# Turning activation blocks for the next product: transposes issued three steps later, the last feed-forward chunk by the tensor engine, one mLSTM block by DRAM

## The chip, the cores and the metric

The kernel runs on one core of one Trainium2 chip. A core has a tensor engine (PE) for matrix products, a vector engine (DVE), a scalar engine (ACT), GpSimd (POOL) and a sync engine (SP) that here only issues transfers. The metric is the time of one execution in microseconds (us), as the median of repeated runs. The kernel before takes 1747.4 us, and its three runs lie between 1746.92 and 1747.4 us.

## The reference

One decoder layer on 256 tokens of width 2048, in fp32. Every product below is against weights that are read once from memory.

```python
def hybrid_mixer(h, ...):
    mq, mk, mv, mo, mi, mf, dq, dk, dv, gm, gd = split_in(h @ w_in)
    ...                                              # conv and silu on mq, mk
    hm = jax.nn.sigmoid(mo) * head_rmsnorm(mlstm_chunkwise(q, k, v, ig, lf), m_norm_w)
    hd = head_rmsnorm(diff_attention(dq, dk, dv, lam), d_norm_w) * (1.0 - lam_init)
    y = jax.nn.sigmoid(gm) * (hm @ w_bm) + jax.nn.sigmoid(gd) * (hd @ w_bd)
    return y @ w_out
def swiglu(h, w_gate, w_up, w_down):
    return (jax.nn.silu(h @ w_gate) * (h @ w_up)) @ w_down
def reference(x, ...):
    x = x + hybrid_mixer(rmsnorm(x, attn_norm_w), ...)
    x = x + swiglu(rmsnorm(x, ffn_norm_w), w_ffn_gate, w_ffn_up, w_ffn_down)
    return rmsnorm(x, final_norm_w)
```

## The kernel before

**Products.** A number is kept as two parts, hi and lo, and a product is three matmuls: hi by hi, hi by lo, lo by hi (`three`, L175; its lines L177 to L179 are the matmuls of the profile). Weights arrive by DMA in pieces of 1 MB (`wr`, four buffers). ACT casts half a piece to its hi part (`wh`, L331, or L478 in the plain products) and DVE subtracts to get the lo part (`wl`, L335 or L479); both rings have five buffers, and a split is written into the program four units ahead of the product that reads it (`AHEAD`). Some products come in pairs that share seven instead of eight block products (`Pair`, L341; the banks P1 to P8): `bd` (hd by w_bd), `wo` (y by w_out), `fgu` (gate and up) and `fd` (down). DVE adds up raw weights for those (L323), and `quarters` (L407) puts the outputs together with DVE (L410).

**Turned activations.** A product reads its activations with features on the partitions. They are computed with tokens on the partitions, so each block of 512 features (a chunk) is turned before the product that reads it. The chunk is kept in a `Split` (`hmT`, `yT`, `x1T`, and `gT0`, `gT1`, `gT2` for the three parts of the feed-forward, which have 4, 4 and 3 chunks). `across_task` (L202) chooses the way by the chunk's kind:

- a kind in `TURN` (L46) goes by `turn_task` (L249): two DVE stream transposes of 32x32 blocks (L255), one POOL DMA to DRAM (L260), four POOL DMAs back (L265), then the hi part by ACT (L278, or L282 and L283 where a scale is applied) and the lo part by DVE (L279 or L284);
- any other kind goes by `transpose_task` (L210): a wait of two steps, four PE transposes of 128x128 into a bank (L187), hi by ACT (L190, or L196 with a scale), lo by DVE (L191 or L199), a wait of two steps, and the same for the second half.

Before, the PE way is taken by `hm0` (the first mLSTM block, which `bm` reads much later), by `ylast` (chunks 2 and 3 of y, read by wo0), by `x1last` (chunks 2 and 3 of x1, read by fgu0), and by `glast` (chunk 2, the last, of gT2, read by fd20). The last chunk (3) of gT0 and of gT1, read by fd00 and fd10, has the kind `g` and goes by DRAM (L1140).

**What sets the order.** The whole program is written out by hand, engine by engine, and each engine runs its list in order. Side work is held in generators of class `Side` (L89). `side.tick()` moves each of them on by one step; `Pair.run` (L383) ticks after every six matmuls of a pair, so a step is six matmuls of the main product. Generators of one lane run one after another; `ylast`, `x1last` and `glast` chunks share the lane `tr`. Before a product reads a chunk, `side.until` ticks as often as it takes for the chunk's last instruction to be in the program. The number after `yield` in `transpose_task` is thus what places the PE transposes between the matmuls.

Of the kernel before, what the change touches and what calls it, by code (L numbers as in the profile page):

```python
# [42 lines left out]
)  # L43
N_WARM = (6, 2)
SHORT = set()
TURN = {"q0", "k0", "hm1", "hm2", "hm3", "dq", "dk", "hd0", "hd1", "hd2", "hd3", "y", "x1", "g"}  # L46


@with_exitstack
def hybrid_block(ctx, tc, x, attn_norm_w, w_in, conv_w, conv_b, b_igate, b_fgate, mlstm_norm_w,  # L50
# [17 lines left out]
    def c4(shape, name, dt=F32):  # L68
        return c4p.tile(shape, dt, tag="c4", name=name)
# [8 lines left out]
    def t2(shape, name, dt=F32):  # L78
        return smp.tile(shape, dt, tag="t2", name=name, bufs=N_T2)
# [9 lines left out]
    class Side:  # L89
# [10 lines left out]
        def across(self, lane, kind, *rest):  # L100

            gen = across_task(kind, *rest)
            if kind in TURN and kind not in SHORT:
                self.spawn(gen)
# [28 lines left out]
    side = Side()  # L133
# [47 lines left out]
    def transpose_half(src, dst, g, pr, scale_col=None):  # L181

        hi, lo = dst.hi[g], dst.lo[g]
        ps = bank("ps_tr", (P, 2, S))
        for j in range(2):
            for tt in range(TT):
                nc.tensor.transpose(ps[:, j, tt * P:(tt + 1) * P], src(tt, 2 * pr + j), ident)  # L187
        if scale_col is None:
            h = hi[:, 2 * pr:2 * pr + 2]
            nc.scalar.copy(out=h, in_=ps)  # L190
            nc.vector.tensor_tensor(out=lo[:, 2 * pr:2 * pr + 2], in0=ps, in1=h.bitcast(F32),  # L191
                                    op=ALU.subtract)
        else:
            for j in range(2):
                k = 2 * pr + j
                nc.scalar.activation(out=hi[:, k], in_=ps[:, j], func=AF.Identity, scale=scale_col(4 * g + k))  # L196
            for j in range(2):
                k = 2 * pr + j
                nc.vector.scalar_tensor_tensor(out=lo[:, k], in0=ps[:, j], scalar=scale_col(4 * g + k),  # L199
                                               in1=hi[:, k].bitcast(F32), op0=ALU.mult, op1=ALU.subtract)  # L200

    def across_task(kind, tile, dst, g, scale_col=None, rate=2):  # L202
        if kind in SHORT:
            yield from turn_short_task(tile, dst, g, scale_col, rate)
        elif kind in TURN:
            yield from turn_task(tile, dst, g, scale_col, rate)
        else:
            yield from transpose_task(lambda tt, j: tile[:, tt, j * P:(j + 1) * P], dst, g, scale_col)

    def transpose_task(src, dst, g, scale_col=None):  # L210
        yield 2
        dst.alloc(g)
        transpose_half(src, dst, g, 0, scale_col)
        yield 2
        transpose_half(src, dst, g, 1, scale_col)
        dst.ready[g] = True
# [11 lines left out]
    def turn_short_task(src, dst, g, scale_col=None, rate=2):  # L228
        yield 1
        t = c4([P, 4, S], "turned")  # L230
        yield from turn(src, t, rate)
        hi, lo = dst.alloc(g)
        for k in range(0, 4, 2):
            if scale_col is None:
                nc.scalar.copy(out=hi[:, k:k + 2], in_=t[:, k:k + 2])
                nc.vector.tensor_tensor(out=lo[:, k:k + 2], in0=t[:, k:k + 2], in1=hi[:, k:k + 2].bitcast(F32),
                                        op=ALU.subtract)
            else:
                for j in (k, k + 1):
                    sc = scale_col(4 * g + j)  # L240
                    nc.scalar.activation(out=hi[:, j], in_=t[:, j], func=AF.Identity, scale=sc)
                    nc.vector.scalar_tensor_tensor(out=lo[:, j], in0=t[:, j], scalar=sc, in1=hi[:, j].bitcast(F32),
                                                   op0=ALU.mult, op1=ALU.subtract)
            if k == 0:
                yield
        yield
        dst.ready[g] = True
# [159 lines left out]
    def quarters(pair):  # L407

        def op(o, i0, i1, op_):
            nc.vector.tensor_tensor(out=o, in0=i0, in1=i1, op=op_)  # L410
        ps = pair.banks
        yield from pair.after("P3", 2)
        s3, u, v, x = (t2([P, 512], f"q{i}") for i in range(4))
        nc.scalar.copy(out=s3, in_=ps["P3"])
        yield from pair.after("P6", 2)
        op(u, s3, ps["P6"], ALU.subtract)
        op(v, u, ps["P4"], ALU.add)
        yield
        op(x, v, ps["P5"], ALU.subtract)
        op(u, ps["P5"], u, ALU.subtract)  # L420
        for t, c, b, o, op_ in ((0, 0, "P1", s3, ALU.add), (1, 0, "P7", v, ALU.subtract),
                                (0, 1, "P2", u, ALU.add), (1, 1, "P8", x, ALU.add)):
            yield from pair.after(b, 2)
            op(o, ps[b], o, op_)
            yield t, c, o
# [357 lines left out]
    def conv_task(tok, ft0, dst):  # L783
# [3 lines left out]
        dst.alloc(0)  # L787
        if dst.name in TURN:
            t = c4([P, 4, S], "turned")
            yield from turn(tok, t)  # L790
        for pr in range(2):
            y = t2([P, 2, S], "cv")
            if dst.name in TURN:
                ps = t[:, 2 * pr:2 * pr + 2]
# [278 lines left out]
    x1 = []  # L1073
# [52 lines left out]
    def gate_up_post(gT, i):  # L1126
        def task(pair):
            g = c4([P, TT, 512], "g")
            for got in quarters(pair):
                if got is None:  # L1130
                    yield
                    continue
                t, c, q = got
                yield
                if c == 0:
                    nc.scalar.activation(out=g[:, t], in_=q, func=AF.Silu, scale=r2(t))
                else:
                    nc.vector.scalar_tensor_tensor(out=g[:, t], in0=q, scalar=r2(t), in1=g[:, t],
                                                   op0=ALU.mult, op1=ALU.mult)
            side.across("tr", "g" if i < 2 or len(gT.hi) > 3 else "glast", g, gT, i, None, 4)  # L1140
        return task

    ss2 = small([P, TT, 4], "ss2", bufs=1)
# [106 lines left out]
    for pi, (f0, f1) in enumerate(parts):  # L1250
        gT = Split(f1 - f0, f"gT{pi}", {0})
# [81 lines left out]
```

## Time and profile before

| what | value |
|---|---|
| median of three runs | 1747.4 us (1746.92 to 1747.4) |
| the profiled execution | 1748.35 us |
| its span in the trace | 1746.5 us |
| PE busy | 1722.0 us, 99% of the span |
| DVE busy | 1317.7 us, 75% |
| ACT busy | 933.1 us, 53% |
| DMA, mean | 210 GB/s |

The span is the time from the first to the last instruction of the trace; 1.85 us of the profiled execution lie around it. A busy PE is not one at its peak, since matmuls overlap and their ends are modelled; where matmuls follow each other without a wait, the distance of their starts is the price of one. The chain that ended last is PE for 87% of the span, DVE for 7%.

### The profile page before, as it was taken

Reading aid. Unit: us, or ns where it says so; the run is one execution under the profiler, and the core shown is the slowest. Engines: PE = TensorE matmul, PEld = TensorE weight load, DVE = VectorE, ACT = ScalarE, POOL = GpSimd, SP = SyncE. Lnnn points to the kernel's source line nnn. Section 1 sums busy time; section 2 is a strip of 40 time slices with the busy share of each in tenths; the row PEclk is TensorE's granted clock in tenths of the full one; section 3 lists DMA queues with packets and bytes.
Section 4 is the critical chain, followed back from the end, with each engine's and each line's share of the span. In section 5 each row is a group of like instructions: output and inputs, shape, how many; then the busy total and the mean of one; then the engine's idle time right before and its main releaser. Section 6 shows DMA issues by size and latency. Waiting matters only on the chain.

```text
span 1746.5 us, 20555 instructions
## 1 busy us (share of the span) xinstructions
PE 1722.0 (99%) x7753; PEld 1422.3 (81%) x7753; DVE 1317.7 (75%) x1744; ACT 933.1 (53%) x1207; POOL 88.5 (5%) x180
## 2 busy tenths in 40 slices
PE   9999999999999999999998999999999999999998
PEld 7888888888888888888887878888788887788876
DVE  6876876655556677675689898888788888788896
ACT  7555555654345565565545565455444555445453
POOL 1000000000000111010010100000000000000000
PEclk9999999999999999999999999999999999999999
DMA  9656566666777768676685766676566676567663
GB/s 303 199 178 191 159 181 192 201 216 218 218 218 213 228 204 244 200 228 196 220 265 192 229 206 217 201 246 228 183 202 217 201 239 227 177 194 225 207 232 107
DMA packets 180772, 366.72 MB, mean 210 GB/s; under 512 B 10032, under 2 KB 11712, under 8 KB 180672
## 3 DMA queue, kind: packets, MB, share of 16 engines
q1 hardware_dynamic: 170320, 332.88, 60.0%
q0 software_dynamic: 10320, 32.52, 6.2%
q8 instruction: 61, 1.00, 0.2%
q14 instruction: 39, 0.32, 0.0%
q10 hardware_dynamic: 32, 0.01, 0.0%
HBM read 345.97 MB, written 19.40 MB: 209 GB/s over the span
## 4 chain that ended last, share of the span: by engine, by line
PE 87%; DVE 7%; issue 2%; DMA 2%; ACT 2%; SPq 0%; POOL 0%; DVEq 0%; ACTq 0%; POOLq 0%
PE acc_fgu_P L178 7%; PE acc_fgu_P L179 7%; PE acc_fgu_P L177 7%; PE acc_fd_P L179 4%; PE acc_fd_P L177 4%; PE acc_fd_P L178 4%; DVE wl_fgu L335 2%; PE acc_mo L177 2%; PE acc_mv L177 2%; PE acc_gm L177 2%; PE acc_dq L177 2%; PE acc_dk L179 2%; PE acc_dk L177 2%; PE acc_gd L177 2%; PE acc_mo L179 2%
## 5 line engine op out<-in xcount | busy, mean ns | idle before, releaser
L331 ACT CAST wh_fgu<-wr_fgu 128x1024 fp32r<-128x1024 f32 x209 | 213.7, 1050 | 162.9 <-PE acc_fgu_P L179 80.9
L335 DVE TENSOR_TENSOR wl_fgu<-wr_fgu,wh_fgu 128x1024 fp32r<-128x1024 f32 x209 | 251.8, 1221 | 60.4 <-ACT wh_fgu L331 57.0
L178 PE MATMUL acc_fgu_P<-wl_fgu,x1Th 128*128 128x512 f32 x594 | 231.4, 390 | 1.7 <-DVE wl_fgu L335 1.7
L177 PE MATMUL acc_fgu_P<-wh_fgu,x1Th 128*128 128x512 f32 x594 | 231.4, 390 | 0.0
L179 PE MATMUL acc_fgu_P<-wh_fgu,x1Tl 128*128 128x512 f32 x594 | 231.2, 389 | 0.0
L331 ACT CAST wh_fd<-wr_fd 128x1024 fp32r<-128x1024 f32 x91 | 93.9, 1050 | 93.1 <-PE acc_fd_P L179 63.8
L335 DVE TENSOR_TENSOR wl_fd<-wr_fd,wh_fd 128x1024 fp32r<-128x1024 f32 x91 | 110.0, 1222 | 40.7 <-ACT wh_fd L331 39.9
L178 PEld LDWEIGHTS acc_fgu_P<-wl_fgu,x1Th 128*128 128x128 f32 x594 | 111.5, 188 | 25.8 <-DVE wl_fgu L335 3.0
L179 PEld LDWEIGHTS acc_fgu_P<-wh_fgu,x1Tl 128*128 128x128 f32 x594 | 111.5, 188 | 23.2
L177 PEld LDWEIGHTS acc_fgu_P<-wh_fgu,x1Th 128*128 128x128 f32 x594 | 111.5, 188 | 23.1
L260 POOL DMA_DIRECT2D across<-turned x29 | 16.4, 566 | 1317.1 <-DVE turned L255 1317.1
L265 POOL DMA_DIRECT2D across<-across x116 | 63.5, 554 | 123.4 <-DMA across<-turned 79.5
L479 DVE TENSOR_TENSOR wl_bm<-wr_bm,wh_bm 128x1024 fp32r<-128x1024 f32 x32 | 39.2, 1225 | 40.5 <-ACT wh_bm L478 40.5
L479 DVE TENSOR_TENSOR wl_dv<-wr_dv,wh_dv 128x1024 fp32r<-128x1024 f32 x32 | 38.8, 1219 | 37.8 <-ACT wh_dv L478 37.8
L331 ACT CAST wh_bd<-wr_bd 128x1024 fp32r<-128x1024 f32 x38 | 39.7, 1053 | 40.9 <-PE acc_bd_P L179 24.7
L479 DVE TENSOR_TENSOR wl_gm<-wr_gm,wh_gm 128x1024 fp32r<-128x1024 f32 x32 | 39.2, 1223 | 28.8 <-ACT wh_gm L478 28.7
L479 DVE TENSOR_TENSOR wl_gd<-wr_gd,wh_gd 128x1024 fp32r<-128x1024 f32 x32 | 39.1, 1224 | 27.8 <-ACT wh_gd L478 27.6
L479 DVE TENSOR_TENSOR wl_dq<-wr_dq,wh_dq 128x1024 fp32r<-128x1024 f32 x32 | 39.2, 1225 | 27.3 <-ACT wh_dq L478 27.0
L335 DVE TENSOR_TENSOR wl_bd<-wr_bd,wh_bd 128x1024 fp32r<-128x1024 f32 x38 | 46.1, 1220 | 18.1 <-ACT wh_bd L331 17.4
L478 ACT CAST wh_bm<-wr_bm 128x1024 fp32r<-128x1024 f32 x32 | 33.7, 1054 | 46.7 <-PE acc_bm L179 39.9
L478 ACT CAST wh_dq<-wr_dq 128x1024 fp32r<-128x1024 f32 x32 | 33.7, 1053 | 43.4 <-PE acc_dv L179 16.6
L479 DVE TENSOR_TENSOR wl_mv<-wr_mv,wh_mv 128x1024 fp32r<-128x1024 f32 x32 | 38.9, 1222 | 23.0 <-ACT wh_mv L478 22.7
(453 smaller groups left out, 4682.1 us busy)
## 6 DMA issues: line engine op xcount, KB each, us to landing
wr_fgu<-in_w_ffn_gate_dram SPq DMA_DIRECT2D x44, 1024.0 KB, 5.2
wr_fgu<-in_w_ffn_up_dram SPq DMA_DIRECT2D x44, 1024.0 KB, 5.2
wr_fd<-in_w_ffn_down_dram SPq DMA_DIRECT2D x44, 1024.0 KB, 5.3
wr_mo<-in_w_in_dram SPq DMA_DIRECT2D x16, 1024.0 KB, 5.4
wr_mv<-in_w_in_dram SPq DMA_DIRECT2D x16, 1024.0 KB, 5.4
wr_gm<-in_w_in_dram SPq DMA_DIRECT2D x16, 1024.0 KB, 5.6
wr_bm<-in_w_branch_m_dram SPq DMA_DIRECT2D x16, 1024.0 KB, 5.2
wr_dq<-in_w_in_dram SPq DMA_DIRECT2D x16, 1024.0 KB, 5.7
```

Source lines behind the costliest of these rows:

```text
L177: nc.tensor.matmul(o, lhsT=a[0], rhs=b[0], start=first, stop=False)
L178: nc.tensor.matmul(o, lhsT=a[0], rhs=b[1], start=False, stop=False)
L179: nc.tensor.matmul(o, lhsT=a[1], rhs=b[0], start=False, stop=last)
L260: nc.gpsimd.dma_start(out=d.rearrange("a f b n -> (a f) (b n)"), in_=y.rearrange("p b k t s -> p (b k t s)"))
L265: nc.gpsimd.dma_start(out=t[32 * b:32 * b + 32].rearrange("p a u s -> p a (u s)"), in_=d[:, :, b].rearrange("a f n -> f a n"))
L331: nc.scalar.copy(out=hi, in_=r)
L335: nc.vector.tensor_tensor(out=lo, in0=r, in1=hi.bitcast(F32), op=ALU.subtract)
L478: nc.scalar.copy(out=hi[:, i:i + step], in_=r)
L479: nc.vector.tensor_tensor(out=lo[:, i:i + step], in0=r, in1=hi[:, i:i + step].bitcast(F32), op=ALU.subtract)
```

## The change

Three edits. `hm0` joins the kinds that are turned by way of DRAM, so its eight PE transposes go. `transpose_task` waits five steps instead of two before the first half; it concerns every chunk that PE turns. And the last chunk of gT0 and gT1 changes from `g` to `glast`, so it is turned by PE: eight transposes in fd00 and eight in fd10, while two trips by DRAM go. For gT2 the kind stays (its chunk 2 was `glast` and is). The two arguments that fall away at the end of the call were defaults or not read by either task.

```diff
-TURN = {"q0", "k0", "hm1", "hm2", "hm3", "dq", "dk", "hd0", "hd1", "hd2", "hd3", "y", "x1", "g"}
+TURN = {"q0", "k0", "hm0", "hm1", "hm2", "hm3", "dq", "dk", "hd0", "hd1", "hd2", "hd3", "y", "x1", "g"}
...
     def transpose_task(src, dst, g, scale_col=None):
-        yield 2
+        yield 5
         dst.alloc(g)
         transpose_half(src, dst, g, 0, scale_col)
         yield 2
...
-            side.across("tr", "g" if i < 2 or len(gT.hi) > 3 else "glast", g, gT, i, None, 4)
+            side.across("tr", "g" if i < len(gT.hi) - 1 else "glast", g, gT, i)
```

What this does to the order of instructions is shown at three places. The numbers behind names are those of the program's buffers; they count up as the program is written, so one and the same buffer is shifted by a few between the two programs.

PE in wo0, before, where the first half of chunk 2 of y (`sgd2`) is turned (`yTh1` and `yTl1` are chunk 1 of y, turned long ago):

```order
L178 MATMUL acc_wo0_P3_7836<-wl_wo0_7757,yTh0_7654 128x512
L179 MATMUL acc_wo0_P3_7836<-wh_wo0_7756,yTl0_7655 128x512
L187 MATMUL ps_tr_7845<-ident_82,sgd2_6980 128x128 x4
L177 MATMUL acc_wo0_P1_7810<-wh_wo0_7775,yTh1_7687 128x512
L178 MATMUL acc_wo0_P1_7810<-wl_wo0_7776,yTh1_7687 128x512
```

The same chunk's first half in the changed program, with what precedes and follows it on PE:

```order
L178 MATMUL acc_wo0_P8_7873<-wl_wo0_7789,yTh1_7688 128x512
L179 MATMUL acc_wo0_P8_7873<-wh_wo0_7788,yTl1_7689 128x512
L187 MATMUL ps_tr_7879<-ident_82,sgd2_6981 128x128 x4
L177 MATMUL acc_wo0_P2_7869<-wh_wo0_7788,yTh1_7688 128x512
L178 MATMUL acc_wo0_P2_7869<-wl_wo0_7789,yTh1_7688 128x512
```

The half stands 18 matmuls later, three steps, among matmuls of the next weight pieces.

PE in fd20, before, ahead of the first reader of chunk 2 of gT2 (`gT2h2`, `gT2l2`; both halves stand further up, 13 and 32 rows above the first reader):

```order
L178 MATMUL acc_fd20_P4_13530<-wl_fd20_13451,gT2sh0_12993 128x512
L179 MATMUL acc_fd20_P4_13530<-wh_fd20_13450,gT2sl0_12994 128x512
L177 MATMUL acc_fd20_P1_13397<-wh_fd20_13460,gT2h2_13473 128x512
L178 MATMUL acc_fd20_P1_13397<-wl_fd20_13461,gT2h2_13473 128x512
L179 MATMUL acc_fd20_P1_13397<-wh_fd20_13460,gT2l2_13474 128x512
```

The same stretch of PE in the changed program (`g_13111` is the chunk before it is turned):

```order
L178 MATMUL acc_fd20_P4_13524<-wl_fd20_13452,gT2sh0_12994 128x512
L179 MATMUL acc_fd20_P4_13524<-wh_fd20_13451,gT2sl0_12995 128x512
L187 MATMUL ps_tr_13536<-ident_82,g_13111 128x128 x4
L177 MATMUL acc_fd20_P1_13398<-wh_fd20_13461,gT2h2_13503 128x512
L178 MATMUL acc_fd20_P1_13398<-wl_fd20_13462,gT2h2_13503 128x512
L179 MATMUL acc_fd20_P1_13398<-wh_fd20_13461,gT2l2_13504 128x512
```

The second half now stands directly ahead of the chunk's first reader, and the first half 13 rows above it.

DVE in fd20, before, around the lo part of the chunk's two halves (L191):

```order
L335 TENSOR_TENSOR wl_fd20_13461<-wr_fd20_13431,wh_fd20_13460 128x1024
L191 TENSOR_TENSOR gT2l2_13474<-ps_tr_13475,gT2h2_13473 128x512
L335 TENSOR_TENSOR wl_fd20_13489<-wr_fd20_13363,wh_fd20_13488 128x1024
L323 TENSOR_TENSOR wr_fd20_13288<-wr_fd20_13288,wr_fd20_13363 128x1024
L335 TENSOR_TENSOR wl_fd20_13499<-wr_fd20_13431,wh_fd20_13498 128x1024
L191 TENSOR_TENSOR gT2l2_13474<-ps_tr_13511,gT2h2_13473 128x512
```

The same stretch of DVE in the changed program:

```order
L335 TENSOR_TENSOR wl_fd20_13462<-wr_fd20_13432,wh_fd20_13461 128x1024
L335 TENSOR_TENSOR wl_fd20_13481<-wr_fd20_13364,wh_fd20_13480 128x1024
L323 TENSOR_TENSOR wr_fd20_13289<-wr_fd20_13289,wr_fd20_13364 128x1024
L335 TENSOR_TENSOR wl_fd20_13491<-wr_fd20_13432,wh_fd20_13490 128x1024
L191 TENSOR_TENSOR gT2l2_13504<-ps_tr_13505,gT2h2_13503 128x512
L335 TENSOR_TENSOR wl_fd20_13519<-wr_fd20_13289,wh_fd20_13518 128x1024
```

The lo part of the first half stands behind three more DVE instructions than before.

## Rows read from the trace of the kernel before

**Rows 1.** The page: span; busy us (share of span) and instructions of each engine.

```profile
span 1746.5 us, 20555 instructions
PE 1722.0 (99%) x7753; PEld 1422.3 (81%) x7753; DVE 1317.7 (75%) x1744; ACT 933.1 (53%) x1207; POOL 88.5 (5%) x180
```

**Rows 2.** Waits of PE: line waited for, us in total, times, longest.

```profile
PE ps_tr L187 <- DVE sgd L1094: 3.1, 1, 3.1
...
PE acc_fd_P L177 <- ACT gT0h L278: 1.7, 1, 1.7
PE acc_fd_P L177 <- ACT gT1h L278: 1.7, 1, 1.7
...
PE ps_tr L187 <- DVE x L1108: 1.6, 1, 1.6
PE ps_tr L187 <- DVE g L1138: 1.3, 1, 1.3
...
PE acc_fd_P L179 <- DVE gT1l L279: 0.6, 1, 0.6
PE acc_fd_P L179 <- DVE gT0l L279: 0.6, 1, 0.6
```

**Rows 3.** Timeline, PE, turning hm0: start us, us, engine line op, xcount.

```profile
205.30 0.39 PE L179 MATMUL acc_mo<-wh_mo,xtl 128*128 128x512 f32 x1
205.53 0.60 PE L187 MATMUL ps_tr<-ident,hraw 128*128 128x128 f32 x4
...
206.20 0.40 PE L178 MATMUL acc_mo<-wl_mo,xth 128*128 128x512 f32 x1
```

**Rows 4.** Timeline, POOL: hm1 leaves for DRAM; in brackets its idle time before.

```profile
257.29 0.74 POOL L260 DMA_DIRECT2D across<-turned  x1 [225.67 <-DVE turned L255]
```

**Rows 5.** DMA issues of that trip, 255 to 285 us: KB each, us to landing.

```profile
across<-turned POOLq DMA_DIRECT2D x1, 512.0 KB, 6.7
across<-across POOLq DMA_DIRECT2D x4, 128.0 KB, 6.6
```

**Rows 6.** Readers of hmTh: ns min/median/max, first and last start us.

```profile
L177 PE MATMUL acc_bm<-wh_bm,hmTh x128: 389/389/389, 386.0 to 472.4; 128*128 128x512 f32 x128
```

**Rows 7.** Timeline, PE in fd00: from before chunk 3's first read to after it.

```profile
1221.75 0.40 PE L177 MATMUL acc_fd_P<-wh_fd,gT0sh 128*128 128x512 f32 x1
...
1231.69 0.40 PE L177 MATMUL acc_fd_P<-wh_fd,gT0h 128*128 128x512 f32 x1
```

**Rows 8.** Stretches: busy us of PE, PEld, DVE, ACT, POOL; PE clock, DMA share, GB/s.

```profile
934.00:940.00 6.00, 2.90 (x16) 2.18 (x15) 5.93 (x8) 1.60 (x3) 0.00 (x0) 1.00 0.52 170
...
1226.00:1231.00 5.00, 4.67 (x13) 3.69 (x14) 0.88 (x2) 0.65 (x1) 0.00 (x0) 0.66 0.63 211
```

**Rows 9.** Timeline, PE in wo0: the first half, and a later weight part's reader.

```profile
935.50 0.27 PE L187 MATMUL ps_tr<-ident,sgd 128*128 128x128 f32 x1
...
946.80 0.39 PE L178 MATMUL acc_wo_P<-wl_wo,yTh 128*128 128x512 f32 x1
```

**Rows 10.** Timeline, DVE in wo0: that weight part.

```profile
943.98 1.22 DVE L335 TENSOR_TENSOR wl_wo<-wr_wo,wh_wo 128x1024 fp32r<-128x1024 f32 x1
```

**Rows 11.** Timeline, DVE in fgu0: a weight part behind the sums of x1.

```profile
1030.63 1.22 DVE L335 TENSOR_TENSOR wl_fgu<-wr_fgu,wh_fgu 128x1024 fp32r<-128x1024 f32 x1
```

**Rows 12.** Timeline, PE in fgu0: that weight part's first reader.

```profile
1034.91 0.39 PE L178 MATMUL acc_fgu_P<-wl_fgu,x1Th 128*128 128x512 f32 x1
```

**Rows 13.** Timeline, PE in fd20: the reader of the first half's lo part.

```profile
1689.88 0.39 PE L179 MATMUL acc_fd_P<-wh_fd,gT2l 128*128 128x512 f32 x1
```

**Rows 14.** Timeline, DVE in fd20: a weight part, then a half's lo part.

```profile
1690.27 1.22 DVE L335 TENSOR_TENSOR wl_fd<-wr_fd,wh_fd 128x1024 fp32r<-128x1024 f32 x1
1691.40 0.68 DVE L191 TENSOR_TENSOR gT2l<-ps_tr,gT2h 128x512 fp32r<-128x512 f32 x1
```

**Rows 15.** Timeline, ACT in fd20: hi part of the second half.

```profile
1688.37 0.57 ACT L190 CAST gT2h<-ps_tr 128x512 fp32r<-128x512 f32 x1
```

## The prediction

> **What bounds the kernel now.** I read the page first, then the waits of PE, then the timelines around each wait. The page shows PE busy for 1722.0 of 1746.5 us; the next engine, DVE, for 1317.7 [rows 1]. So a change of this kind pays in two ways only: fewer instructions on PE, or fewer places where PE stands. The waits of PE [rows 2] name the places, and they are few. Three are the first halves that PE turns: it reaches the transposes before DVE has finished the block, and waits 3.1 us in wo0 (`sgd`), 1.6 us in fgu0 (`x`) and 1.3 us in fd20 (`g`). Two are the last chunks of gT0 and gT1 that come by DRAM: 1.7 us for the hi part and 0.6 us for the lo part, in fd00 and again in fd10. After these two the clock of PE falls: between 1226 and 1231 us the granted clock is 0.66 on average [rows 8], which is (1 - 0.66) x 5 x 2 = 3.4 us at the lower level, 1.2 instead of 2.4 GHz, so about 1.7 us lost. From 934 to 940 us, around the longest single wait, it stays at 1.00 [rows 8].
>
> The prices. What follows a matmul starts 0.23 us after it (205.30 and 205.53) [rows 3]. From the four transposes at 205.53 to the second matmul behind them are 0.67 us [rows 3]; less one matmul, a turned half costs PE 0.44 us, a chunk 0.88 us.
>
> **The change part by part.**
>
> *hm0 by DRAM.* Two halves leave PE: -0.9 us. What comes is two DVE transposes, five POOL transfers, and about as many ACT and DVE passes as go. The trip itself is hidden: the one of hm1 took 6.7 us out and 6.6 us back [rows 5], some 16 us with the four issues, POOL had been idle for 225 us before it [rows 4], and the first reader of hmT starts at 386.0 us [rows 6], 180 us after hm0 is turned. If that cover were gone the price would be the trip, 16 us; the only one who could feel it early is ACT, which keeps its order and has the weight casts behind the hi part, and the order puts that part ten or more steps after the last transfer. Taken at -0.9.
>
> *Last chunk of gT0 and gT1 by PE.* From 1221.75 to 1231.69 us are 9.94 us [rows 7] for 24 matmuls, which at 0.23 are 5.5: 4.4 us are lost there, 2.3 by the two waits, 1.7 by the clock, the rest by restarts. In the changed order the second half of the chunk stands 48 matmuls, 11 us, ahead of its first reader, so ACT and DVE have ample time for the parts. What goes is 4.4, what comes is 0.88: -3.5 us in fd00, and the same in fd10, whose waits are the same. The ends: -4.4 if the halves fell into other gaps, and 0 if the lo part came late again. I take -3.5 for each; 11 us is far from the two DVE instructions that would have to fit.
>
> *Three steps later in fgu0.* Three steps are 18 matmuls, 4.1 us, more than the wait of 1.6 us. What is late next is DVE. The weight part that DVE makes behind the sums of x1 is done at 1030.63 + 1.22 = 1031.85 [rows 11], and its first reader, at 1034.91 before [rows 12], comes 1.6 us earlier for the wait and 0.44 for the half that has moved behind it: 1032.87. That is 1.0 us of slack, so the whole wait is gained: -1.6 us (ends: -1.6 and -0.6).
>
> *Three steps later in wo0.* Here the wait of 3.1 us does not go, it moves. DVE is busy without a break there: 5.93 of 6 us [rows 8]. In its order, the sums of y's last two chunks come first, then the weight part at 943.98 to 945.20 [rows 10]. Its reader stood at 946.80 [rows 9], 1.6 us behind. Without the 3.1 us, and with the second half now behind this reader, PE arrives at 946.80 - 3.1 - 0.44 = 943.3 and waits about 2 us. It goes on at 945.25 instead of 946.80, with one half (0.44) still to do: net 1.55 - 0.44 = -1.1 us. The ends: -3.1 if DVE gets there earlier, 0 if the later halves' parts hold DVE up once more.
>
> *Three steps later in fd20.* The wait of 1.3 us goes, and a worse one comes. The chunk is wanted right away: in the new order its second half stands directly ahead of the first reader. The lo part of its first half (L191) now stands behind two more weight parts and a weight sum. Before, the second of those parts started at 1690.27 and took 1.22 [rows 14]; the L191 that stood ahead of it (0.6 us of queue) is gone, so it ends at about 1690.9, and the L191 (0.68 [rows 14]) at about 1691.5. The hi part takes the place on ACT that the second half's had, and ends at 1688.94 [rows 15]. So the first reader waits shortly for ACT, and the third matmul, which reads the lo part, starts at 1691.55 where it started at 1689.88 [rows 13], with as many transposes ahead of it as before: +1.7 us. The ends: -1.3 (no new wait) and +2.5 (the second half's part late as well).
>
> *The clock.* New waits stand in wo0 (2 us, single) and in fd20 (one for ACT, one of 2 us for DVE, two or three matmuls apart). Single waits of 3.1 and 1.6 us did not bring the clock down [rows 2, 8], the close pair in fd00 did. By the nearest row fd20 is a pair, wo0 is not: +1.7 us in fd20, 0 in wo0. The other ends are 0 and +1.7.
>
> The sum: -0.9 - 3.5 - 3.5 - 1.6 - 1.1 + 1.7 + 1.7 = -7.2 us. Against the profiled execution (1748.35 us, span 1746.5) this gives 1741.15; the median of the runs is 0.95 us lower, so against 1747.4 it gives **1740.2 us**.
>
> On transposes there is a rule that speaks against this change. In all stretches before, halves turned by PE left the clock at 1.00 (934 to 940 us holds one) [rows 8]. The Trainium skill, page "TensorE: Matmul & The Clock Gate", section "Part 4: PE-mode transpose", says that a transpose does not count as busy for the clock in the way that a matmul does, and gives about 275 ns for one in a kernel. By that price a half would cost 1.1 us instead of 0.44, and the sum would be, as an estimate from that page, about 1.3 us less of a gain; the row has the duration, so it is used. What the first part of the rule would do is the fourth rival.
>
> **The rivals.**
>
> 1. *The clock holds in fd20.* The same sum without the last term: -8.9 us, 1738.5. For it: the single waits of before left the clock alone, and this pair is uneven. Against: the pair in fd00 and fd10 did not, both times.
>
> 2. *DVE is late twice.* The clock falls in wo0 as well (+1.7), or the second half's lo part in fd20 is late too: about 1741.9. For it: DVE has no break in either place.
>
> 3. *The moved transposes cost nothing.* DVE keeps ahead: wo0 -3.1, fd20 -1.3, no clock term: -0.9 - 7.0 - 1.6 - 3.1 - 1.3 = -13.9, 1733.5. Against: the ends of the DVE rows above.
>
> 4. *Transposes draw the clock down.* With eight more of them in fd00 and fd10, one fall of 1.7 us each stays there: 1740.2 + 3.4 = 1743.6. Against: the clock of 1.00 around the halves before. By the rule above this would happen; no row bears it out.
>
> 5. *Slower: the lo parts come late at all five places.* The mechanism is that of fd20: the half is turned so close ahead of its reader that L191 or L199 stands behind weight parts. In fd20 it gives 0.8 + 2.1 us of waits, some restarts and 1.7 of clock, about 4.8. Five times that is 24.0; before, the five places lost 3.1 + 1.6 + 1.3 + 4.4 + 4.4 = 14.8, and the transposes add 1.76 - 0.88 = 0.9. Result: 24.0 - 14.8 + 0.9 = +10.1, 1757.5. It turns into a loss from 2.8 us per place on. For it: DVE is the next engine in line in all five. Against: the order leaves 48 matmuls between turning and reading in fd00 and fd10, and in wo0 and fgu0 the chunk's readers come later than the weight parts.
>
> That the change does not do what it says I leave out: the order shows all three edits.
>
> **How the numbers follow.** Chances: forecast 0.42, rival 1 0.27, rival 2 0.14, rival 3 0.04, rival 4 0.06, rival 5 with its half ways 0.07. Forecast and rivals 1 and 2 hold 0.83 and lie between 1738.5 and 1741.9; with an error of a few tenths to one us in the DVE ends of wo0 and fgu0 and the -0.9 of hm0 on each side, the range is **1736.8 to 1743.0**. A measurement here can tell 0.2%, 3.5 us, from no change. Faster by more than that (below 1743.9) are the forecast, rivals 1 to 3 and a part of rival 4: 0.88. Within it: the rest of rival 4 and the milder half of rival 5: 0.08. Slower: 0.04.
>
> **What would show it.** In the profile of the changed kernel the waits of PE should have no line for `ps_tr` (three before) and none for `gT0h`, `gT1h`, `gT0l`, `gT1l`; new lines should be L178 on `wl_wo` with about 2 us and, in fd20, L179 on `gT2l` from L191 with about 2 us, with a short wait on L190 ahead of it. The granted clock should be 1.00 from 1215 to 1232 us, and fall, if at all, behind the waits of fd20 near 1690. Eight transposes of `hraw` should be gone from PE, and sixteen of `g` be there, at 0.44 us a half. The forecast is wrong if DVE's weight parts in wo0 end at another time than the order and the durations say, if the lo parts in fd00 come late, or if a wait appears at a place that PE passes without one today.

## The result, and the profile after

The changed kernel takes 1738.5 us (median of five runs, 1735.5 to 1740.5), the kernel before took 1747.4 us beside it. The ratio is 0.9947, with a 95% interval from 0.9933 to 0.9962: faster by 0.4 to 0.7%, about 9 us. The forecast was 1740.2 us, with a range from 1736.8 to 1743.0; rival 1, the same sum without a fall of the clock in fd20, gave 1738.5. The profiled execution took 1739.11 us, its span is 1737.4 us, 9.1 us less than before.

First the page of the changed kernel (span; busy us, share of the span and instructions of each engine), which answers to [rows 1]:

```profile
span 1737.4 us, 20556 instructions
PE 1719.1 (99%) x7761; PEld 1420.3 (82%) x7761; DVE 1316.7 (76%) x1740; ACT 934.2 (54%) x1209; POOL 85.8 (5%) x175
```

PE has eight instructions more (eight transposes of `hraw` gone, sixteen of `g` come) and is done 9 us earlier. So the gain is not work taken away; it is waits, and the falls of PE's clock behind them. The waits of PE, which answer to [rows 2] (line waited for, us in total, times, longest):

```profile
PE acc_wo_P L178 <- DVE wl_wo L335: 2.2, 2, 2.0
PE acc_fd_P L179 <- DVE gT2l L191: 2.0, 1, 2.0
PE acc_fgu_P L178 <- DVE wl_fgu L335: 1.7, 3, 0.6
PE acc_fd_P L178 <- DVE wl_fd L335: 1.2, 1, 1.2
...
PE acc_bd_P L178 <- DVE wl_bd L335: 0.2, 1, 0.2
```

All seven lines of [rows 2] are gone: no `ps_tr`, no `gT0` or `gT1`. Two new ones of 2.0 us stand where the prediction put them, on `wl_wo` in wo0 and on `gT2l` in fd20. The 1.2 us for `wl_fd` in fd20 are larger than the 0.8 us that the prediction's fifth rival counted there, and the ACT wait that it named does not show. The wait for `wl_bd` is 0.2 us here, which nobody had forecast. In the trace of before it was the second longest of all, though [rows 2] do not show it and the prediction has no term for it:

```profile
PE acc_bd_P L178 <- DVE wl_bd L335: 1.9, 1, 1.9
```

The stretches of the changed kernel in which the chunks that now come by PE are first read (us, then busy us and instructions of PE, PEld, DVE, ACT, POOL; granted clock of PE, DMA share, GB/s), against the 0.66 of [rows 8]:

```profile
1219.00:1224.00 5.00, 5.00 (x23) 4.01 (x23) 2.82 (x4) 2.56 (x4) 0.00 (x0) 1.00 0.70 222
1475.00:1480.00 5.00, 5.00 (x24) 4.01 (x23) 2.98 (x3) 2.57 (x4) 0.00 (x0) 1.00 0.73 233
```

PE is busy for all of the 5 us, at the clock of 2.4 GHz.

To see where the time went I matched the two traces matmul by matmul, in the order of the program, and took the difference of the start times at the first matmul of each product. The difference of two neighbours is what a product gained or lost:

| stretch | forecast, us | first profile after, less before, us |
|---|---|---|
| start to mk0 | 0 | +0.4 |
| mo2 (hm0) | -0.9 | -0.95 |
| bd2 (`wl_bd`) | 0 | -1.65 |
| wo0 | -1.1 | -0.95 |
| wo2 | 0 | +0.5 |
| fgu0 | -1.6 | -1.8 |
| fd00 | -3.5 | -3.5 |
| fd10 | -3.5 | -3.45 |
| fd20 | +1.7 | +2.4 |
| clock in fd20 | +1.7 | 0 |
| sum | -7.2 | -9.1 |

(The sum is that of the whole spans; the rounded rows add up to -9.0.) The first row is scatter: over all thirteen profiles mk0 starts up to 0.8 us earlier or 0.4 us later than in the first trace of before, and 0.75 us earlier in the second profile of the kernel before.

### The profile page after: what moved, and what is told of

It reads as the page before. It is cut to its first block, busy times and chain, and to the rows that moved or that the text cites. A ratio compares the mean times of both kernels' runs of the same rounds, so it can differ in the third digit from the quotient of the medians.

```text
span 1737.4 us, 20556 instructions
## 1 busy us (share of the span) xinstructions
PE 1719.1 (99%) x7761; PEld 1420.3 (82%) x7761; DVE 1316.7 (76%) x1740; ACT 934.2 (54%) x1209; POOL 85.8 (5%) x175
## 4 chain that ended last, share of the span: by engine, by line
PE 86%; issue 5%; DVE 5%; DMA 2%; ACT 1%; POOL 0%; SPq 0%; DVEq 0%; ACTq 0%; POOLq 0%
PE acc_fgu_P L178 8%; PE acc_fgu_P L179 8%; PE acc_fgu_P L177 8%; PE acc_fd_P L177 4%; PE acc_fd_P L179 4%; PE acc_fd_P L178 4%; PE acc_mv L177 2%; PE acc_mo L177 2%; PE acc_gm L177 2%; PE acc_dq L177 2%; PE acc_dk L179 2%; PE acc_dk L177 2%; PE acc_mo L179 2%; PE acc_mo L178 2%; PE acc_dk L178 2%
## 5 line engine op out<-in xcount | busy, mean ns | idle before, releaser
L265 POOL DMA_DIRECT2D across<-across x112 | 61.3, 554 | 126.2 <-DMA across<-turned 76.1
L479 DVE TENSOR_TENSOR wl_dq<-wr_dq,wh_dq 128x1024 fp32r<-128x1024 f32 x32 | 39.2, 1225 | 27.3 <-ACT wh_dq L478 27.0
L331 ACT CAST wh_wo<-wr_wo 128x1024 fp32r<-128x1024 f32 x38 | 39.4, 1052 | 33.7 <-PE acc_wo_P L179 15.2
```

What stands on the lines that cost most here:

```text
L265: nc.gpsimd.dma_start(out=t[32 * b:32 * b + 32].rearrange("p a u s -> p a (u s)"), in_=d[:, :, b].rearrange("a f n -> f a n"))
L331: nc.scalar.copy(out=hi, in_=r)
L479: nc.vector.tensor_tensor(out=lo[:, i:i + step], in0=r, in1=hi[:, i:i + step].bitcast(F32), op=ALU.subtract)
```

## The experiments

The theory: each edit acts in the places that the prediction named, by the waits that it named; the clock adds falls of 1.7 us behind some of the waits. Two things were open: where bd2's 1.65 us come from, and whether a fall of the clock is a property of the kernel.

**One edit alone: hm0 by DRAM.**

```diff
-TURN = {"q0", "k0", "hm1", "hm2", "hm3", ...
+TURN = {"q0", "k0", "hm0", "hm1", "hm2", "hm3", ...
```

> Only the first edit: hm0 goes by DRAM, all else as before. Theory: two turned halves leave PE, 0.44 us each, so the time is 0.9 us lower (about 1746.5), the shift is there from mo3 on and stays the same up to wo0; the wait for wl_bd in bd2 (1.9 us before, 0.2 us with all three edits) has nothing to do with it and comes out anywhere between 0 and 2 us. Rival: the trip by DRAM, or the order that goes with it, is what shortened that wait; then this kernel shows a wl_bd wait of about 0.2 us and is 2.6 us faster (about 1744.8).

Measured: 1744.7 us against 1746.9 us, ratio 0.9988 (0.9979 to 0.9997). The interval is 0.5 to 3.7 us of gain, so the time alone does not tell the forecast (0.9) from the rival (2.6). By the trace, mo2 gives 0.95 us, as forecast, and the trip, 14.8 us from 209.25 to 224.03, is felt by nobody. bd2 gives 2.1 us more, since its wait is not there at all; wo2 takes 1.4 of them back, behind a wait of 1.1 us for a weight part. Four of its waits:

```profile
PE ps_tr L187 <- DVE sgd L1094: 3.1, 1, 3.1
PE acc_fd_P L177 <- ACT gT1h L278: 2.1, 1, 2.1
...
PE acc_fd_P L177 <- ACT gT0h L278: 1.7, 1, 1.7
...
PE acc_wo_P L178 <- DVE wl_wo L335: 1.1, 1, 1.1
```

Taken alone the missing wait for `wl_bd` speaks for the rival (the trip shortened it). The next run decides.

**One edit alone: five steps.**

```diff
     def transpose_task(src, dst, g, scale_col=None):
-        yield 2
+        yield 5
```

> Only the second edit: five steps ahead of the first half instead of two; hm0 by PE and chunk 3 of gT0 and gT1 by DRAM as before. Theory: wo0 -1.0, fgu0 -1.8, fd20 +2.4, nothing in fd00 and fd10 (both still wait 1.7 + 0.6 us and lose the clock): -0.4 us in sum, about 1747.0, without the wl_bd wait -2 more. Rival: the later steps are the main part of the gain and fd20 costs little: -3 to -4 us, about 1744.

Measured: 1747.0 us against 1746.9 us, ratio 1.0 (0.9991 to 1.0008). The later steps by themselves are worth nothing here. By the trace fgu0 gains 1.8 us and fd20 gives 1.6 back; wo0 loses 0.6, since the clock falls there behind the new wait, where it gained 0.95 in the first profile of the changed kernel without a fall. Its waits show the exchange: the `ps_tr` lines are gone, and the new ones are there with the size that they have in the changed kernel.

```profile
PE acc_wo_P L178 <- DVE wl_wo L335: 2.0, 1, 2.0
PE acc_fd_P L179 <- DVE gT2l L191: 2.0, 1, 2.0
PE acc_fd_P L177 <- ACT gT0h L278: 1.7, 1, 1.7
PE acc_fd_P L177 <- ACT gT1h L278: 1.7, 1, 1.7
```

This kernel turns hm0 by PE, and yet has no wait for `wl_bd`. So that wait does not hang on hm0, and the rival of the run before falls. The clock, in the same two places that had both lost it before (stretches of this kernel, columns as above):

```profile
1222.00:1227.00 5.00, 4.73 (x21) 3.89 (x22) 1.79 (x3) 1.76 (x2) 0.00 (x0) 1.00 0.62 214
1479.00:1484.00 5.00, 4.39 (x13) 3.20 (x12) 1.55 (x3) 0.13 (x1) 0.00 (x0) 0.66 0.72 256
```

Both stretches stand behind the same pair of waits, 1.7 and 0.6 us. In fd00 the clock stays, in fd10 it falls; in the first trace of before it fell in both.

**One edit alone: the last chunk of gT0 and gT1 by PE, at two steps.**

```diff
-            side.across("tr", "g" if i < 2 or len(gT.hi) > 3 else "glast", g, gT, i, None, 4)
+            side.across("tr", "g" if i < len(gT.hi) - 1 else "glast", g, gT, i)
```

> Only the third edit: chunk 3 of gT0 and gT1 by PE, at two steps; hm0 by PE. Theory: the gain in fd00 and fd10 comes from the way, not from the steps: -3.5 us each, -7.0 in sum, about 1740.4, with no PE wait for g in fd00 and fd10 because DVE has g finished before PE gets there even at two steps, and the clock stays at 1.00 there. Rival: at two steps PE comes before DVE has finished g, as in fd20, and waits 1.3 us in each place: -4.4 us, about 1743.

Measured: 1742.5 us against 1746.9 us, ratio 0.9977 (0.9967 to 0.9987), 4.0 us by the ratio. The time is the rival's, the mechanism is the theory's. By the trace fd00 and fd10 gain 3.4 us each, and the first half in fd00 does not wait: DVE writes the last part of `g` from 1202.70 for 0.74 us, and PE turns it at 1204.09 (timelines of DVE and PE: start us, us).

```profile
1202.70 0.74 DVE L1138 SCALAR_TENSOR_TENSOR g<-q,rs_x,g 128x512 f32<-128x512 f32 x1
...
1204.09 0.60 PE L187 MATMUL ps_tr<-ident,g 128*128 128x128 f32 x4
```

The `g` that its waits name stands in fd20. What the forecast of 7.0 us had left out is on the other side of the comparison: it took the clock of the first trace of before, which had fallen in both places, for that of every run. Where it does not fall, fd00 loses 2.3 us of waits and the restarts, and the edit is worth 1.8 us there, not 3.5. In fd10 it fell in all four traces that have the waits, so 3.4 us stand there. And this run had a fall of its own, in wo0, behind the 3.1 us that had left the clock alone before:

```profile
PE ps_tr L187 <- DVE sgd L1094: 3.1, 1, 3.1
PE ps_tr L187 <- DVE g L1138: 1.7, 1, 1.7
...
938.00:943.00 5.00, 4.94 (x16) 3.97 (x17) 4.86 (x8) 2.03 (x4) 0.00 (x0) 0.66 0.26 97
```

**The changed kernel once more.** No edit.

> The changed kernel itself once more, with a second profile. Theory: the waits of PE are the same to 0.1 us in wo0 (2.0, L178 on wl_wo) and fd20 (1.2 and 2.0), but whether the granted clock falls behind one of them is not a property of the kernel: it may fall here in wo0 or fd20 where it stayed at 1.00 in the first profile, 1.6 to 1.7 us each time. Rival: the clock is fixed by the waits; then it stays at 1.00 throughout, as in the first profile, and the differences between runs have another cause.

Measured: 1740.4 us against 1745.7 us, ratio 0.9962 (0.9949 to 0.9974). The waits in fd20 are there again (2.0 us, and 0.9 instead of 1.2 us); the one in wo0 is not the same, against the expectation. The clock fell in bd2 and in fd20, where the first profile of the same kernel had 1.00:

```profile
923.84:927.25 3.41, 3.41 (x10) 2.67 (x9) 3.41 (x4) 1.98 (x3) 0.00 (x0) 0.50 0.34 91
1681.60:1685.00 3.40, 3.40 (x10) 2.65 (x9) 2.81 (x3) 0.77 (x1) 0.00 (x0) 0.50 1.05 405
```

So the last term of the forecast, a fall in fd20, is no error of kind: it happens in one of the three profiles with the wait of 2.0 us there (the five-step kernel above is the third), and fd20 then loses 3.7 us instead of 2.4. The two profiles differ in bd2 as well:

```profile
PE acc_bd_P L178 <- DVE wl_bd L335: 1.8, 1, 1.8
...
PE acc_wo_P L178 <- DVE wl_wo L335: 0.5, 1, 0.5
```

The wait for `wl_bd` is 1.8 us here and 0.2 in the first profile of the same program. Its source is a transfer: chunk 0 of y, on its way back from DRAM. ACT waits for it (L278), and what follows in the order comes later with it: the sums of the chunk (L157 on DVE, L160 on ACT) and then the weight part that PE will want. First ACT's line of this run, then that of the first profile (in brackets the idle time before and its cause):

```profile
912.84 0.62 ACT L278 CAST yTh<-across 128x512 fp32r<-128x512 f32 x1 [1.85 <-DMA across<-across]
...
912.30 0.62 ACT L278 CAST yTh<-across 128x512 fp32r<-128x512 f32 x1 [1.04 <-DMA across<-across]
```

Counted from the first matmul of bd2 (885.46 and 886.49) these are 27.38 and 25.81 us, and the 1.57 us between them are still there when PE gets to `wl_bd`. Over all thirteen profiles L278 starts 24.98 to 27.94 us after bd2 begins, and the wait follows it: none up to 25.35 us, 0.2 to 0.5 us at 25.8 to 26.0, 1.1 and 1.2 at 26.5 and 26.8, 1.8 to 2.2 from 27.3 on. The kernel before has 27.45 and 25.83 in its two profiles.

That settles bd2: its 1.65 us in the table are a difference between two executions and not a gain of the change. Why the trip back lands later in some of them stays open; the weight piece that lands just before it is late with it (6.9 us from issue to landing here, 5.4 in the first profile).

Of what PE lost in bd2, wo0 pays the fall of the clock back, and not the late landing. From L278 to the first matmul of wo2 are 63.33 us in the first profile and 63.32 here: PE, at half the clock in bd2, comes later to the weight part in wo0 and waits 0.5 us instead of 2.0. Up to there the time is thus set by the work behind that transfer, DVE's in the end, and a fall in bd2 costs nothing. That the lead over before is about the same at the first matmul of fgu0, 2.70 and 2.67 us, is chance: this profile had 1.0 us more of it when bd0 began.

**fd20 at two and at three steps.** In both the waits before the first half are told apart by kind, and only the last chunk of gT2 (`gend`) is changed:

```diff
-            yield from transpose_task(lambda tt, j: ..., dst, g, scale_col)
+            yield from transpose_task(lambda tt, j: ..., dst, g, scale_col, STEPS.get(kind, 5))
...
-            side.across("tr", "g" if i < len(gT.hi) - 1 else "glast", g, gT, i)
+            side.across("tr", "g" if i < len(gT.hi) - 1 else "glast" if i == 3 else "gend", g, gT, i)
```

with `STEPS = {"gend": 2}` in one and `{"gend": 3}` in the other; `transpose_task` takes the number and waits that many steps before the first half.

> All three edits, but the last chunk of gT2 is turned two steps after it is computed, as before the change. Theory: fd20 then loses what it lost before, the wait of 1.3 us for g, and not the 1.2 + 2.0 us: 2.3 us less than the changed kernel, and 0.5 us more than with three steps. Rival: the fd20 loss moves with the arrival of weights and not with the place of the halves; then no difference from the changed kernel beyond 1 us.

> All three edits, but the last chunk of gT2 is turned three steps after it is computed instead of five (before: two). Theory: the wait of 2.0 us in fd20 is there because the lo part (L191) of the first half stands on DVE behind two more weight parts and a weight sum; at three steps it stands where it stood before, so the wait goes, and the wait of 1.3 us for g at two steps goes for the most part too: about 2.8 us less than with five steps, about 1735.7. Rival: what is lost in fd20 hangs on the weight parts themselves (DVE has no break there), and PE waits for wl_fd in place of gT2l: no gain over five steps, about 1738.5.

> The kernel with three steps for the last chunk of gT2 once more, next to the changed kernel on one chip. Theory: 2.8 us below the changed kernel by the trace (fd20 loses 0.4 + 0.3 us instead of 1.2 + 2.0 us and one half's worth of order); the clock, which may or may not fall in wo0 in either, adds up to 1.7 us of scatter to the difference. Rival: no difference beyond 1 us.

Measured on one chip: the changed kernel 1740.4 us, two steps 1736.8 us (ratio to before 0.9942, 0.9929 to 0.9956), three steps 1736.7 us (0.9943, 0.9931 to 0.9956); an earlier job had 1736.9 us for three steps (0.9943, 0.9929 to 0.9956). Both are 3.7 us below the changed kernel in the median. By the traces fd20 loses 2.4 and 3.7 us in the two profiles of the changed kernel, 0.6 us at two steps, and gains 0.5 and 1.5 us at three. These numbers hold a second thing besides the steps: how late DVE comes to the chunk. At two steps alone, fd20 takes anything from 32.55 to 34.59 us in five profiles. The table has two numbers for every profile, both in us from fd20's first matmul: when DVE starts the chunk's first L1138, and when the first matmul of the next product starts (the length of fd20).

| steps | L1138, length of fd20 |
|---|---|
| two | 6.15, 32.55; 6.96, 33.13; 7.86, 34.03; 8.30, 34.49; 8.40, 34.59 |
| three | 5.70, 32.55; 7.37, 32.53; 8.08, 33.26; 8.31, 33.50; 8.35, 33.57 |
| five | 7.56, 35.64; 8.08, 37.73 (the clock falls); 8.31, 36.39 |

Where DVE comes later, fd20 is longer by the same amount, down to 32.5 us, below which it does not get. For the same start of L1138, 8.3 us, it takes 34.5 us at two steps, 33.5 at three and 36.4 at five. So five steps cost 1.9 us against two, and three steps gain 1.0 against two; with DVE at 6.15 us or earlier two and three are the same. The medians, which hold all of these cases and the falls of the clock, do not tell two steps from three. DVE's start in turn goes with a weight piece (`wr_fd`): issued 17.7 us before fd20, it lands 6.1 to 9.0 us later, and L1138 follows the landing by 17.05 to 17.3 us in all thirteen profiles. What makes it land late stays open.

Why, on DVE. First the changed kernel in fd20 (timeline of DVE):

```profile
1675.28 2.50 DVE L335 TENSOR_TENSOR wl_fd<-wr_fd,wh_fd 128x1024 fp32r<-128x1024 f32 x2
1677.70 1.22 DVE L323 TENSOR_TENSOR wr_fd<-wr_fd,wr_fd 128x1024 f32<-128x1024 f32 x1
1678.83 1.22 DVE L335 TENSOR_TENSOR wl_fd<-wr_fd,wh_fd 128x1024 fp32r<-128x1024 f32 x1
1679.97 0.68 DVE L191 TENSOR_TENSOR gT2l<-ps_tr,gT2h 128x512 fp32r<-128x512 f32 x1
```

and PE's wait for it, there:

```profile
1680.71 0.50 PE L179 MATMUL acc_fd_P<-wh_fd,gT2l 128*128 128x512 f32 x1 [1.97 <-DVE gT2l L191]
```

Then the kernel with three steps, second run:

```profile
1672.62 1.22 DVE L335 TENSOR_TENSOR wl_fd<-wr_fd,wh_fd 128x1024 fp32r<-128x1024 f32 x1
1673.76 0.69 DVE L191 TENSOR_TENSOR gT2l<-ps_tr,gT2h 128x512 fp32r<-128x512 f32 x1
1674.36 1.22 DVE L335 TENSOR_TENSOR wl_fd<-wr_fd,wh_fd 128x1024 fp32r<-128x1024 f32 x1
```

At five steps four DVE instructions stand between the weight sum before them and L191, at three steps one. The order of DVE's other instructions is the same. The rival that DVE is too slow as a whole in fd20 would have left the wait in place under another name, and there is none in fd20 in this run. It had the earliest DVE of all (5.70 us); of the two other profiles with three steps, at 8.31 and 8.35 us, each waits 0.4 us there, for `g`. The rival of the arrival of weights holds for what differs between profiles with the same steps, and not for what differs between the steps.

**The sums of y's chunk 3 two steps later, on top of three steps in fd20.**

```diff
-            yield from pair.after(b, 2)
+            yield from pair.after(b, 4 if c and pair.name == "bd2" else 2)
```

> The kernel with three steps for the last chunk of gT2, and the six DVE sums of chunk 3 of y (L410, L1093, L1094) two steps later, behind one weight part of wo0. Theory: the wait of 2.0 us for wl_wo in wo0 is a matter of order on DVE: the weight part stands behind sums that nobody needs yet. With the part ahead of them the wait goes, 2.0 us less than the kernel with three steps, and with the wait any fall of the clock in wo0. Rival: DVE as a whole is too slow from 930 to 960 us (no break there); the wait comes back within wo0 at a later weight part or at yTl, and the time stays within 0.5 us.

Measured: 1734.1 us (1733.7 to 1735.8), ratio to before 0.9931 (0.9919 to 0.9944), 2.6 us below the kernel with three steps on the same chip. In wo0 two weight parts now follow each other ahead of the sums, and the second of the two is what PE had waited for (timeline of DVE):

```profile
935.86 2.35 DVE L335 TENSOR_TENSOR wl_wo<-wr_wo,wh_wo 128x1024 fp32r<-128x1024 f32 x2
938.13 0.68 DVE L410 TENSOR_TENSOR q<-acc_bd_P,q 128x512 f32<-128x512 f32 x1
```

Its waits in bd2 and wo0:

```profile
PE acc_wo_P L179 <- DVE yTl L191: 0.6, 1, 0.6
PE acc_bd_P L178 <- DVE wl_bd L335: 0.4, 1, 0.4
PE acc_wo_P L177 <- ACT yTh L190: 0.2, 1, 0.2
```

The 2.0 us for `wl_wo` are gone, and 0.8 us come back at the chunk's own parts. Whether the stretch got shorter by the rest, the lengths do not show at first sight. From the first matmul of bd0 to that of fgu0 this kernel gains 2.9 us on the first trace of before, the one with two steps in fd20 (which still waits 1.8 us for `wl_wo`) 3.4 us, the changed kernel 2.1 us, the one with three steps 1.8 us; in none of the four does the clock fall there. So I ran both again:

> Three steps for the last chunk of gT2, once more, beside the kernel with the sums of y's chunk 3 two steps later. Theory: from the first matmul of bd0 to that of fgu0 this kernel needs about as long as the one with the later sums when no clock falls in either (DVE's amount of work sets the end there), and up to 1.7 us longer when it falls behind the wait of 2.0 us in wo0; in the median 1 to 2.5 us above the kernel with the later sums. Rival: the later sums save the 2.0 us in every run; then the stretch is 1.5 to 2 us longer here than there, whether the clock falls or not.

> The sums of y's chunk 3 two steps later, once more. Theory: no wait above 1 us in wo0, so the clock stays at 1.00 there; the stretch from bd0 to fgu0 gains little beside a run of the three-step kernel without a fall, and the gain in the median (1 to 2.5 us) is that of falls that don't come. Rival: 2.0 us less in every comparison.

Measured: 1735.2 us with the later sums, 1737.0 us without, on one chip; the ratio to before is 0.9931 (0.9919 to 0.9944) against 0.9937 (0.9925 to 0.9950). The profile without them has the wait of 2.0 us and a fall of the clock in wo0; the one with them has no wait in wo0 and no fall there, but one in bd2, behind 2.2 us for `wl_bd`:

```profile
PE acc_bd_P L178 <- DVE wl_bd L335: 2.2, 1, 2.2
```

It then gains 0.9 us from bd0 to fgu0, as much as the second profile of the changed kernel, which fell in bd2 too (1.05 us). What hides the gain in such comparisons is the landing of y's chunk in bd2. Counted from there, from ACT's L278 to the first matmul of wo2, all thirteen profiles fall into groups (us):

| in wo0 | no fall in wo0 | the clock falls in wo0 |
|---|---|---|
| two steps (as before) | 64.29, 64.28 | 66.07, 65.88 |
| five steps | 63.33, 63.32, 63.32, 63.45 | 65.22, 65.13, 65.07 |
| five steps, sums later | 62.87, 62.86 | none |

So the later sums are worth 0.5 us by themselves, the most that the rival allows, and the rest stays with DVE's amount of work, as the rival has it. A fall in wo0 costs 1.6 to 1.9 us and came in three of the seven profiles with five steps, each time behind a wait of 2.0 us; with the later sums there is no such wait, and no fall in two profiles. A fall in bd2, which one of the four values 63.32 to 63.45 and one of the two lowest have, costs nothing. The granted clock of the single runs agrees: over ten runs each it is 0.9977 without the later sums and 0.9983 with them on average, which is 1.0 us of 1.6 us between the mean times. With its two medians, 1734.1 and 1735.2 us, this kernel is the fastest of those that were run.

**The kernel before once more.** No edit.

> The kernel before once more, with a second profile. Theory: its waits of PE are those of the first profile (3.1 us in wo0, 1.6 in fgu0, 1.3 to 1.8 in fd20, 1.7 + 0.6 in fd00 and in fd10), the wait for wl_bd lies anywhere from 0 to 2 us, and the clock falls behind another choice of them than in the first profile (fd00 and fd10). Rival: the falls belong to the program; then the clock falls in fd00 and fd10 again and nowhere else.

Measured: 1746.1 us against 1747.6 us of its own kind in the same job, ratio 0.9994 (0.9985 to 1.0003). The waits that hang on the order are there again (3.1 in wo0, 1.7 and 0.6 in fd00 and in fd10), and those behind DVE and transfers differ: 0.5 us for `wl_bd` (1.9 in the first profile), 1.2 for x (1.6), 0.4 for g in fd20 (1.3). Two of them:

```profile
PE acc_bd_P L178 <- DVE wl_bd L335: 0.5, 1, 0.5
PE ps_tr L187 <- DVE g L1138: 0.4, 1, 0.4
```

The clock falls in wo0 and in fd10 and stays at 1.00 in fd00 (stretches of wo0, fd00 and fd10, columns as above):

```profile
936.80:940.20 3.40, 3.40 (x10) 2.82 (x11) 3.33 (x5) 2.02 (x3) 0.00 (x0) 0.50 0.37 140
1219.00:1229.00 10.00, 7.70 (x33) 5.67 (x32) 6.02 (x6) 4.40 (x6) 0.00 (x0) 1.00 0.71 244
1482.93:1486.33 3.40, 3.29 (x8) 2.62 (x9) 0.66 (x2) 0.00 (x0) 0.00 (x0) 0.50 0.76 261
```

These are not the places of the first profile. The rival falls.

## Why the prediction was right, point by point

**What bounds the kernel.** Right as far as it went: PE has more instructions than before and the kernel is faster, by the waits and the falls behind them. But the list of waits was not whole. The 1.9 us for `wl_bd` were put at nothing without a reason; they vary from execution to execution and gave 1.65 us in the first profile.

**hm0.** Right, -0.95 us in all nine profiles of kernels that have the edit, and 0 to -0.06 in the others. The way out was slower than hm1's: L265 waited 7.94 us for it.

**fd00 and fd10.** The mechanism is right, the size is right for this pair of traces (-3.5 and -3.45) and in fd00 too large for the median. The step that failed is the 1.7 us of clock in fd00, taken from one profile as if they came every time. Of the four traces with the waits of before, the clock fell in fd00 in one and in fd10 in all; without the fall fd00 takes 1.6 us less. That the halves need not wait for DVE was right at five steps and at two.

**fgu0.** Right, -1.8 against -1.6. Of the slack of 1.0 us 0.7 were left: the weight part ends at 1029.18 in the changed kernel and its first reader starts at 1029.90.

**wo0.** Right, -0.95 against -1.1, and the new wait has the forecast's 2.0 us. The reader of the weight part was to go on at 945.25 in the times of before; it starts at 943.01, with a lead of 2.23 us, which is 945.24. That DVE sets the end was meant for one weight part; the table under the later sums shows it for the whole stretch from the landing in bd2 to wo2.

**fd20.** The sign and the place are right, the term is too small: +2.4 us against +1.7. The lo part was to end at 1691.55 in the times of before; 1679.97 + 0.68 is 1680.65, and with the lead of 11.43 us with which PE enters fd20 it is 1692.1. The prediction took the 0.6 us of the L191 that had moved away off DVE's queue, but DVE came to fd20 0.45 us later against PE than before: the first L1138 of the chunk started at 1678.52 before, and at 1667.53 + 11.43 = 1678.96 here (first the line of before, then that of the changed kernel):

```profile
1678.52 0.75 DVE L1138 SCALAR_TENSOR_TENSOR g<-q,rs_x,g 128x512 f32<-128x512 f32 x1
...
1667.53 0.75 DVE L1138 SCALAR_TENSOR_TENSOR g<-q,rs_x,g 128x512 f32<-128x512 f32 x1
```

Where the three later DVE instructions should have gained 0.6 us, they gained next to nothing. The 0.45 us are not of the change: by the table of fd20 the start of L1138 moves with a weight transfer, and for the same start the cost of five steps is 1.9 us, close to the 1.7 of the forecast.

**The clock.** The reasoning failed. It read from [rows 2] and [rows 8] that single waits leave the clock alone and close pairs bring it down. Over thirteen profiles the clock fell behind the 3.1 us in wo0 in two of four, behind 1.8 to 2.0 us in wo0 in three of six, behind 1.8 us or more in bd2 in two of four, and behind the pair of 1.7 and 0.6 us in five of eight places. Behind the 2.0 us in fd20, the place that the forecast gave a fall, it came in one of three. So the forecast and rival 1 are not two outcomes that exclude each other but two draws of the same kernel.

**The number.** That the sum came so close is in part luck. In the first profile the missing fall in fd20 (1.7 us) and the transfer in bd2 (1.65 us) both made the kernel faster than forecast, and 1.6 us in fd20, wo2 and at the start made it slower; that the median is rival 1's 1738.5 to the digit is chance. The second measurement gains 5.3 us instead of 8.9. Falls of the clock do not tell the two medians apart: the five runs of each have the same granted clock on average, 0.998, and 1740.5 us came with 0.999 and with 0.998, 1738.2 us with 0.999. As an estimate from all profiles, the change is worth about 7 us: 0.95 in mo2, 0.95 in wo0, 1.6 in fgu0 (the wait for x was 1.2 or 1.6 us before), 2.3 in fd00 with a fall in one of four, 3.5 in fd10, less 2.4 in fd20 with a fall in one of three. Falls in wo0 are left out; they came about as often before (two of four profiles) as after (three of seven).

**Rival 4** fell: after the transposes in fd00 and fd10 the clock is 1.00 in all nine profiles that have them there. The rule of the Trainium skill, page "TensorE: Matmul & The Clock Gate", section "Part 4: PE-mode transpose", that transposes do not count as busy in the way that matmuls do, is not contradicted by that, since matmuls stand all around them; no run here shows it. By the price of a half, 0.44 us, the trace keeps to its own number again: 1203.34 to 1204.01 in fd00 is 0.67 us for a half and one matmul, as in [rows 3].

```profile
1203.34 0.60 PE L187 MATMUL ps_tr<-ident,g 128*128 128x128 f32 x4
...
1204.01 0.40 PE L178 MATMUL acc_fd_P<-wl_fd,gT0sh 128*128 128x512 f32 x1
```

One transpose lasts 0.27 us in the trace, but four in a row end after 0.60 us; four times the duration of one, as the prediction reckons in its estimate, is therefore no price of a half.

**Rival 5** had the right mechanism in one place of five. In fd00 and fd10 the distance of 48 matmuls was enough.

## What to carry to other kernels

Where an engine reaches a step before its input is done, moving the step later trades that wait for the next thing in line; look at the queue of the engine that comes after it, since work that moves with the step (here the lo part of a turned half) goes behind whatever was written in between. Give each place the delay that its own producer and its own reader leave room for: five steps gained 1.0 us over two in wo0, made no difference in fd00 and fd10, where the reader is 48 matmuls away, and cost 1.9 us in fd20, where it comes next. And price a fall of the clock by how often it comes in several profiles, not by whether one profile shows it. Where two executions of one program differ, look for the transfer that the slower one waited for, and count the times from its landing: differences of half a microsecond, which the medians hide, then come out.

## What was not expected of the hardware

The same waits in the same program bring PE's granted clock down from 2.4 to 1.2 GHz in one execution and not in another; a fall lasts 3.41 us here. It cost 1.6 us in fd00 and fd20, 1.6 to 1.9 us in wo0, and nothing in bd2, where PE waits for DVE later anyway. It came behind single waits of 1.8 to 3.1 us and behind the pair of 1.7 and 0.6 us. Falls are a part of the scatter of the kernel before (1743.5 to 1748.9 us in ten runs of one job, with a granted clock of 0.998 to 0.995), and not the whole: five of these runs have the same clock, 0.996, and lie between 1745.15 and 1748.69 us.

The rest that the traces show is transfers. In bd2 the four transfers that bring y's chunk back were issued within 0.6 us of the same place in all thirteen profiles and landed 24.9 to 27.9 us after the first matmul; ahead of fd20 a weight piece of 1 MB landed 6.1 to 9.0 us after its issue. Each moves the work behind it by the same amount.
